# Attention weights of two score blocks added into one square ahead of the transpose and taken apart by a mask behind it

## The chip, the cores and the metric

The kernel runs on one core of a Trainium2 chip. The core has a matrix engine (TensorE, PE), which reads its stationary operand with separate weight loads (PEld), a vector engine (VectorE, DVE), an activation engine (ScalarE, ACT), a general engine (GpSimd, POOL), and a sync engine (SyncE, SP) whose queue issues most of the transfers. Each engine works through its own instructions in order and waits for the others at semaphores. The metric is the time of one execution on the device in microseconds (us).

## The reference, cut to what matters

The program is one layer of a hybrid decoder, for a prompt of 512 tokens and 8 samples of 4 tokens, all in f32. One large input projection feeds two branches, an mLSTM and a sliding-window attention; both are gated, projected, added, projected again and normalised. The change touches only the attention of the prompt: 32 query heads of 64 in 4 key groups, a window of 128 tokens, blocks of 128 queries. A query block sees its own key block and the one ahead of it.

```python
def _swa_prompt(q, k, v, slopes, sinks):
    ...
    kk = jnp.concatenate([jnp.pad(kb, pad)[:, :-1], kb], axis=2)
    vv = jnp.concatenate([jnp.pad(vb, pad)[:, :-1], vb], axis=2)
    qi = jnp.arange(WINDOW)[:, None]
    kj = jnp.arange(2 * WINDOW)[None, :]
    dist = qi + WINDOW - kj
    valid = (dist >= 0) & (dist < WINDOW) & ((blk > 0) | (kj >= WINDOW))
    out = _sink_attend(qb, kk, vv, dist, valid, slopes, sinks)
```

`_sink_attend` takes the scaled scores less slope x distance, a softmax over them and one sink logit, and multiplies by the values. From `dist`: query i sees key j of the block ahead only for j > i, and key j of its own block only for j <= i. So of the 256 weights of a query in two blocks, each column j holds one that can differ from zero: in the block ahead if j > i, in the own block if j <= i.

## The kernel before, in words

All large products are made in f32 precision from two halves: a value is split into a rounded high part (cast by ACT, L200 or L243) and the remainder (subtracted by DVE, L201 or L244), and three products hi x hi, hi x lo, lo x hi are summed (L664, L666).

The input projection runs in `paired`: two column tiles of 128 are computed together by seven half products (`half_product`, steps n = 0 to 6), each 24 matmuls of 128 x 272 columns. The loop prepares weights up to three steps ahead (`prepare`: a sum of weight tiles by DVE at L644, or by an accumulating transfer that POOL issues at L642, then the split at L200 and L201 into buffers of two), gathers finished banks (`gather`, L674 to L693, one of them on POOL at L683), and then calls `tick()`, which resumes every side task once. Side tasks are generators: each piece of work up to the next `yield` is written down behind one half product, and `tick` orders the PE instructions of a side task behind the last matmul of that half product. The Tile framework lays the instructions of each engine into one order with a planner that simulates times; preparations and gathers have a higher priority (`AHEAD`), side tasks the plain one.

The attention of the prompt is such a side task (`attentions`, `attention`). It handles two heads (a = 0, 1) at a time, 16 times; one such turn k takes the queries of one pair of projected tiles (`end_qz`) and is spread over the steps of the next two pairs, 14 steps:

- scores (L772, PE) for four query blocks: `s_` is 128 queries x 4 blocks x 256, columns 0 to 127 for the key block ahead, 128 to 255 for the own one; block 0 has only the own one. DVE adds slope x distance (`nb`, scaled by ACT at L762) and finds the minimum (L774);
- exponentials with row sums (L783, ACT), the sink's (L784), the reciprocal (L785, L786, DVE), and the scaling by it (L789, ACT);
- seven transposes a head (L800, PE) of 128 x 128 blocks, in two PSUM tiles of four and three, and their split into `ph` and `pl` (L243, ACT; L244, DVE);
- the product with the values (L810, PE): four pairs of matmuls, whose columns are the own block b and, for b below 3, the block ahead of query block b + 1, so `p_[:, 2b:2b+2]`;
- the sum of its two halves (L813, ACT; L814, DVE) into `hT`, and, after both heads, the product with the gate `sz` (L816, POOL) and the store. `sz` has one buffer and is written for the next turn at L840.

The yields of a turn: one behind each head's scores, one empty, one behind each head's exponentials and scaling, one empty, then for each head transposes, yield, yield, value product, and a last yield ahead of L816.

Of the kernel before, what the change touches and what calls it, by code (L numbers as in the profile page):

```python
# [16 lines left out]
F32R = mybir.dt.float32r  # L17
AF = mybir.ActivationFunctionType
ALU = mybir.AluOpType
# [23 lines left out]
C_ID, C_TRI, C_M8, C_SM, C_SEL, C_M2, C_DIST, C_SB, C_Q, C_N = 0, 128, 256, 264, 296, 328, 330, 586, 718, 846  # L43
# [25 lines left out]
def build(tc, nc, i, o, dbg=None):  # L69
    es = ExitStack()  # L70
    with es:
        _build(tc, nc, i, o, es)


def _build(tc, nc, i, o, es):
# [3 lines left out]
    def pool(stack, name, bufs, space=None, side=None):  # L79
        kw = {"space": space} if space is not None else {}  # L80
        if space is None:
            kw["side"] = side or "right"
            kw["reuse_waits"] = "tile"
        return stack.enter_context(tc.tile_pool(name=name, bufs=bufs, **kw))

    y_p, y_s, C_p, n_p, m_p, kb_p, vb_p, C_s, n_s, m_s, kb_s, vb_s = o
    V, A, G, PE = nc.vector, nc.scalar, nc.gpsimd, nc.tensor
# [13 lines left out]
    def nm(s):  # L101
        count[0] += 1
        return f"{s}_{count[0]}"

    def sm():
        return psB.tile([128, 512], F32, tag="sm", name=nm("sm"))
# [4 lines left out]
    def r32(ap):  # L111
        return ap.bitcast(F32)
# [4 lines left out]
    def blk(ap, n=4):  # L117
        return ap.rearrange("p (b x) -> p b x", b=n)
# [23 lines left out]
    cc = cst.tile([128, C_DIST], F32, name="cc")  # L142
# [3 lines left out]
    ident = cc[:, C_ID:C_ID + 128]  # L146
# [95 lines left out]
    def hilo(src, hi, lo, eng=None):  # L242
        A.copy(hi, src)  # L243
        (eng or V).tensor_tensor(out=lo, in0=src, in1=r32(hi), op=ALU.subtract)  # L244
# [54 lines left out]
    for c0, n in ((0, 256), (256, 256), (512, 512), (1024, 512), (1536, 512)):  # L299
        if c0 < 1536:  # L300
            t_ = xr.tile([128, 4, n], F32, tag=f"x{n}", name=nm("xr"))[:]
        else:
            t_ = act2.tile([128, 8, HT], F32, tag="act", name=nm("xr"))[:].rearrange("p a b -> p (a b)")
            t_ = blk(t_[:, 0:4 * n])
# [10 lines left out]
    for g in range(8):  # L315
        for q in range(2):
            k = g * 2 + q
            pt = sm()
# [408 lines left out]
    bp = {}  # L727

    def open_attention():
        for name, bufs in (("b1", 1), ("bs", 2), ("bt", 1), ("bq", 2), ("bm", 2)):  # L730
            bp[name] = pool(esB, name, bufs)

    def btile(p, shape, tag, dt=F32):
        return bp[p].tile(shape, dt, tag=tag, name=nm(tag))

    def scores_tile():
        return btile("bs", [128, 4, 256], "s")
# [16 lines left out]
    def attention(k, qs, sz, kv):  # L754


        k1, k2, VA = kv
        hT = btile("b1", [128, SEQ], "hT")
        st = []
        for a in range(2):  # L760
            nb = btile("b1", [128, 256], f"nb{a}")
            A.activation(nb[:], state["ca"][:, 0:256], AF.Copy, scale=SLOPES[2 * k + a])  # L762
            s_ = scores_tile()
            mx, mn, sums = (btile("bm", [128, 4], t_) for t_ in ("mx", "mn", "sums"))
            h = slice(2 * k + a, 2 * k + a + 1)
            for j in range(4):
                if j % 2 == 0:
                    pp = sm()
                w0 = 128 if j == 0 else 0
                c0, k0 = (j % 2) * 256, max(j - 1, 0) * 128  # L770
                for n, kx in enumerate((k1, k2)):
                    PE.matmul(pp[:, c0 + w0:c0 + 256], qs[a][:, j * 128:j * 128 + 128], kx[:, k0:k0 + 256 - w0],  # L772
                              start=(n == 0), stop=(n == 1))
                V.tensor_tensor_reduce(s_[:, j, w0:256], pp[:, c0 + w0:c0 + 256], nb[:, w0:256], 1.0, nsinkb[:, h],  # L774
                                       ALU.add, ALU.min, accum_out=mn[:, j:j + 1])
            st.append((s_, mx, mn, sums, h))
            yield
        yield
        for a in range(2):
            s_, mx, mn, sums, h = st[a]  # L780
            for j in range(4):
                sj = s_[:, j, 128 if j == 0 else 0:256]
                A.activation(sj, sj, AF.Exp, bias=mn[:, j:j + 1], scale=-1.0, accum_out=sums[:, j:j + 1])  # L783
            A.activation(mx[:], mn[:], AF.Exp, bias=sinkb[:, h])  # L784
            V.tensor_tensor(out=sums[:], in0=sums[:], in1=mx[:], op=ALU.add)  # L785
            V.reciprocal(sums[:], sums[:])  # L786
            for j in range(4):
                sj = s_[:, j, 128 if j == 0 else 0:256]
                A.activation(sj, sj, AF.Copy, scale=sums[:, j:j + 1])  # L789
            yield  # L790
        yield
        for a in range(2):
            s_ = st[a][0]

            ph, pl = (btile("bt", [128, 7, 128], t_, F32R) for t_ in ("ph", "pl"))
            for m0_, m1_ in ((0, 4), (4, 7)):
                pt = sm()
                for m in range(m0_, m1_):
                    b, own = m // 2, m % 2 == 0
                    PE.transpose(pt[:, (m - m0_) * 128:(m - m0_) * 128 + 128],  # L800
                                 s_[:, b, 128:256] if own else s_[:, b + 1, 0:128], ident)
                n = m1_ - m0_
                hilo(blk(pt[:, 0:n * 128], n), ph[:, m0_:m1_], pl[:, m0_:m1_])
            yield
            yield
            po = sm()
            for b in range(4):
                n = 256 if b < 3 else 128
                for m, p_ in enumerate((ph, pl)):
                    PE.matmul(po[:, b * 128:b * 128 + n], VA[:, b], p_[:, 2 * b:2 * b + n // 128],  # L810
                              start=(b == 0 and m == 0), stop=(b == 3 and m == 1), skip_group_check=True)
            rows_ = slice(a * 64, a * 64 + 64)
            A.copy(hT[rows_], po[64:128])  # L813
            V.tensor_tensor(out=hT[rows_], in0=po[0:64], in1=hT[rows_], op=ALU.add)  # L814
        yield
        G.tensor_tensor(out=hT[:], in0=sz[:, 0:SEQ], in1=hT[:], op=ALU.mult)  # L816
        nc.sync.dma_start(d_bra[k][:, 0:SEQ], hT[:])

# [36 lines left out]
    def attentions():  # L855
# [10 lines left out]
        with tc.issue_after(state["load"].ins):  # L866
            nc.sync.dma_start(state["ca"][:], i["consts"][:, C_DIST:C_DIST + 388])
        open_attention()
        state["open"] = True
        spawn(old_rows())  # L870
        for k in range(16):
            if k % 4 == 0:
                kv = kv_head(k // 4)
            while k not in waiting:
                yield
            yield
            yield
            yield from attention(k, *waiting.pop(k), kv)
            state["done"] = k + 1
# [487 lines left out]
    ph = wA1.tile([128, 1280], F32R, name="ph")  # L1367
    pl = wA1.tile([128, 1280], F32R, name="pl")
# [526 lines left out]
```

## Time and profile before

| What | us |
|---|---|
| median of 3 runs | 2493.77 |
| lowest and highest | 2491.63, 2494.89 |
| the profiled execution | 2497.55 |
| its span, first to last instruction | 2495.7 |
| PE busy | 2453.8 |
| DVE busy | 1817.8 |
| ACT busy | 1244.1 |
| POOL busy | 373.1 |

The profile is of one execution. The busy time of an engine is the time in which at least one of its instructions runs; matmuls overlap, so the mean duration of one is longer than the spacing from one to the next. In a row of groups stand the line, engine and operation, output and inputs, the shapes and the number of instructions, then the merged busy time in us and the mean duration in ns, and the idle time of the engine just ahead of them with what ended it. In a row in order of time stand the start, the duration in us (from the first start to the last end, if several are merged, xN), and in brackets an idle time ahead of it.

### The profile page before, as it was taken

The page shows a single profiled execution, that of the slowest core. Times are in us where ns is not written, and L with a number is a line of the kernel's source. Part 1 is how long each engine was busy: PE and PEld are TensorE (multiplying, and loading weights), DVE is VectorE, ACT ScalarE, POOL GpSimd, SP SyncE. Part 2 cuts the span into 40 slices and gives each one's busy share as a digit, 9 for nine tenths or more (in the row PEclk, how much of TensorE's full clock was granted, in tenths as well). Part 3 has the DMA queues.
Part 4 walks back from the last instruction along what each step waited for, and adds up shares of the span by engine and source line. Part 5 has one row for each costly group of instructions (what it writes and reads, how often), then busy time and mean ns, then how long its engine had stood idle before and what let it go on. Part 6 is the DMA issues. An engine that isn't in the chain of part 4 may idle for free. (4 is left out here: it accounts for less than half of the span.)

```text
span 2495.7 us, 48772 instructions
## 1 busy us (share of the span) xinstructions
PE 2453.8 (98%) x19542; PEld 2394.0 (96%) x19542; DVE 1817.8 (73%) x2785; ACT 1244.1 (50%) x2033; POOL 373.1 (15%) x376
## 2 busy tenths in 40 slices
PE   8999999999999999999999999999999999999997
PEld 8999999999999999989999999999999999999997
DVE  7867677677677677777878788878855654666667
ACT  6457677667667665433433444444633333334431
POOL 2111121121111111121021121210000000110111
PEclk9999999999999999999999999999999999999999
DMA  6677666656666655468678677677755546788776
GB/s 166 154 185 187 150 151 159 158 144 163 153 152 156 151 128 151 106 204 243 205 216 243 167 232 240 188 225 226 251 171 172 189 149 205 198 229 258 213 220 190
DMA packets 557172, 464.71 MB, mean 186 GB/s; under 512 B 45328, under 2 KB 454080, under 8 KB 556688
## 3 DMA queue, kind: packets, MB, share of 16 engines
q1 hardware_dynamic: 540048, 402.07, 54.4%
q0 software_dynamic: 15696, 57.15, 11.8%
q8 instruction: 154, 2.52, 0.4%
q10 hardware_dynamic: 1200, 2.36, 0.3%
q14 instruction: 74, 0.61, 0.1%
HBM read 319.06 MB, written 96.31 MB: 166 GB/s over the span
## 5 line engine op out<-in xcount | busy, mean ns | idle before, releaser
L200 ACT CAST wh<-raw 128x1024 fp32r<-128x1024 f32 x632 | 661.9, 1048 | 814.6 <-PE bank L664 663.8
L201 DVE TENSOR_TENSOR wl<-raw,wh 128x1024 fp32r<-128x1024 f32 x632 | 778.9, 1234 | 222.7 <-ACT wh L200 203.4
L664 PE MATMUL bank<-xk,wh 128*128 128x272 f32 x2336 | 325.0, 290 | 0.9 <-DVE ev L689 0.9
L644 DVE TENSOR_TENSOR raw<-raw,raw 128x1024 f32<-128x1024 f32 x238 | 304.5, 1280 | 17.3 <-DMA raw<-in_w_in 8.2
L664 PEld LDWEIGHTS bank<-xk,wh 128*128 128x128 f32 x2336 | 304.3, 189 | 4.2 <-issue 2.6
L683 POOL TENSOR_TENSOR ev<-p,ev 128x272 f32<-128x272 f32 x82 | 124.8, 1522 | 674.1 <-ACT ev L682 613.7
L666 PE MATMUL bank<-xk,wl 128*128 128x272 f32 x1168 | 172.4, 288 | 0.8 <-DVE wl L201 0.8
L664 PE MATMUL bank<-s1h,wh 128*128 128x272 f32 x656 | 169.1, 291 | 0.2 <-ACT wh L200 0.2
L664 PE MATMUL bank<-n3h,wh 128*128 128x272 f32 x656 | 169.1, 289 | 0.0
L664 PE MATMUL bank<-n2h,wh 128*128 128x272 f32 x656 | 168.2, 289 | 0.6 <-ACT wh L200 0.6
L664 PE MATMUL bank<-s4h,wh 128*128 128x272 f32 x656 | 168.3, 290 | 0.1
L664 PE MATMUL bank<-n3l,wh 128*128 128x272 f32 x656 | 167.9, 287 | 0.0
L664 PE MATMUL bank<-n2l,wh 128*128 128x272 f32 x656 | 167.5, 287 | 0.0
L664 PE MATMUL bank<-s1l,wh 128*128 128x272 f32 x656 | 167.2, 287 | 0.0
L664 PE MATMUL bank<-s4l,wh 128*128 128x272 f32 x656 | 167.0, 287 | 0.0
L666 PEld LDWEIGHTS bank<-xk,wl 128*128 128x128 f32 x1168 | 156.6, 188 | 1.1 <-DVE wl L201 1.0
L664 PE MATMUL bank<-a11h,wh 128*128 128x272 f32 x584 | 150.8, 290 | 2.6 <-ACT wh L200 2.5
L209 PE MATMUL bank<-bh,wl 128*128 128x272 f32 x704 | 148.5, 291 | 4.7 <-DVE wl L201 4.7
L664 PE MATMUL bank<-a11l,wh 128*128 128x272 f32 x584 | 149.6, 289 | 0.0
L209 PE MATMUL bank<-bh,wh 128*128 128x272 f32 x704 | 148.8, 290 | 0.0
L209 PE MATMUL bank<-bl,wh 128*128 128x272 f32 x704 | 148.6, 290 | 0.0
L664 PEld LDWEIGHTS bank<-n3h,wh 128*128 128x128 f32 x656 | 123.3, 188 | 1.9 <-issue 1.4
(488 smaller groups left out, 5515.4 us busy)
## 6 DMA issues: line engine op xcount, KB each, us to landing
raw<-in_w_in SPq DMA_DIRECT2D x296, 512.0 KB
raw<-raw POOLq DMA_DIRECT2D x90, 512.0 KB, 5.0
C<-in_state_mlstm_C SPq DMA_DIRECT2D x32, 1024.0 KB
out<-C SPq DMA_DIRECT2D x64, 512.0 KB
raw<-in_w_proj_a SPq DMA_DIRECT2D x32, 512.0 KB
raw<-in_w_proj_m SPq DMA_DIRECT2D x32, 512.0 KB
raw<-in_w_out SPq DMA_DIRECT2D x32, 512.0 KB
d_v<-ev SPq DMA_DIRECT2D x16, 272.0 KB
```

Of the source, the lines that this page charges most:

```text
L200: A.copy(wh[:, k:k + n], raw[:, k:k + n])
L201: V.tensor_tensor(out=wl[:, k:k + n], in0=raw[:, k:k + n], in1=r32(wh[:, k:k + n]), op=ALU.subtract)
L209: PE.matmul(ps[f][:, :w], a[:, kk], b(k, c, w), start=(k == 0 and n == 0), stop=(k == 15 and n == 2))
L644: V.tensor_tensor(out=w[out][:], in0=w[a][:], in1=w[b][:], op=ALU.add)
L664: PE.matmul(ps, wh[:, k], x(p, k), start=(first and k == 0 and p == 0), stop=False, skip_group_check=True)
L666: state["end"] = PE.matmul(ps, wl[:, k], x(0, k), start=False, stop=(k == 7), skip_group_check=True)
L683: G.tensor_tensor(out=c22, in0=p1, in1=c11, op=ALU.subtract)
```

## The change

Ahead of the scaling, POOL adds the weights of the key block ahead to those of the own block, for query blocks 1 to 3: one square of 128 x 128 a query block. Only that square is scaled, and only four transposes a head are made, into one PSUM tile. Behind them, ACT writes the rounded copy `fh` and DVE the remainder `fl` over the free halves of `s_`. A tile of ones and zeros (`upper`, one exponential of the triangle constant when the pools are opened) takes them apart: the product with it is the own block's part (f x 1 or f x 0), and the difference of the square and that product is the part of the block ahead. POOL does this for `fh`, DVE for `fl`, into tiles `P`, of which there are three buffers for the four of a turn. The tiles go to the same value products as before. The copies of the distances for the two heads (`nb`) now share one buffer. The transposes of both heads now stand in two steps that follow each other, and each head's value product one step later than before; the last yield ahead of the gate's product is gone.

```diff
-        for name, bufs in (("b1", 1), ("bs", 2), ("bt", 1), ("bq", 2), ("bm", 2)):
+        for name, bufs in (("b1", 1), ("bs", 2), ("bt", 3), ("bq", 2), ("bm", 2)):
             bp[name] = pool(esB, name, bufs)
+        upper = bp["upper"] = btile("b1", [128, 128], "upper")
+        A.activation(upper[:], cc[:, C_TRI:C_TRI + 128], AF.Exp)
...
-            nb = btile("b1", [128, 256], f"nb{a}")
+            nb = btile("b1", [128, 256], "nb")
...
+            G.tensor_tensor(out=s_[:, 1:4, 128:256], in0=s_[:, 1:4, 0:128], in1=s_[:, 1:4, 128:256], op=ALU.add)
             A.activation(mx[:], mn[:], AF.Exp, bias=sinkb[:, h])
             V.tensor_tensor(out=sums[:], in0=sums[:], in1=mx[:], op=ALU.add)
             V.reciprocal(sums[:], sums[:])
             for j in range(4):
-                sj = s_[:, j, 128 if j == 0 else 0:256]
+                sj = s_[:, j, 128:256]
                 A.activation(sj, sj, AF.Copy, scale=sums[:, j:j + 1])
             yield
         yield
+        ps_ = []
         for a in range(2):
             s_ = st[a][0]
-
-            ph, pl = (btile("bt", [128, 7, 128], t_, F32R) for t_ in ("ph", "pl"))
-            for m0_, m1_ in ((0, 4), (4, 7)):
-                pt = sm()
-                for m in range(m0_, m1_):
-                    b, own = m // 2, m % 2 == 0
-                    PE.transpose(pt[:, (m - m0_) * 128:(m - m0_) * 128 + 128],
-                                 s_[:, b, 128:256] if own else s_[:, b + 1, 0:128], ident)
-                n = m1_ - m0_
-                hilo(blk(pt[:, 0:n * 128], n), ph[:, m0_:m1_], pl[:, m0_:m1_])
-            yield
+            pt = sm()
+            for b in range(4):
+                PE.transpose(pt[:, b * 128:b * 128 + 128], s_[:, b, 128:256], ident)
+            fh, fl = s_[:, :, 0:128], s_[:, :, 128:256]
+            A.copy(fh.bitcast(F32R), blk(pt[:]))
+            V.tensor_tensor(out=fl.bitcast(F32R), in0=blk(pt[:]), in1=fh, op=ALU.subtract)
+
+            up = bp["upper"][:].unsqueeze(1).to_broadcast([128, 4, 128])
+            both = []
+            for e, f in ((G, fh), (V, fl)):
+                p_ = btile("bt", [128, 7, 128], "P", F32R)
+                e.tensor_tensor(out=p_[:, 0:7:2], in0=f, in1=up, op=ALU.mult)
+                e.tensor_tensor(out=p_[:, 1:7:2], in0=f[:, 1:4], in1=r32(p_[:, 2:7:2]), op=ALU.subtract)
+                both.append(p_)
+            ps_.append(both)
+            yield
+        for a in range(2):
             yield
             po = sm()
             for b in range(4):
                 n = 256 if b < 3 else 128
-                for m, p_ in enumerate((ph, pl)):
+                for m, p_ in enumerate(ps_[a]):
                     PE.matmul(po[:, b * 128:b * 128 + n], VA[:, b], p_[:, 2 * b:2 * b + n // 128],
                               start=(b == 0 and m == 0), stop=(b == 3 and m == 1), skip_group_check=True)
             rows_ = slice(a * 64, a * 64 + 64)
             A.copy(hT[rows_], po[64:128])
             V.tensor_tensor(out=hT[rows_], in0=po[0:64], in1=hT[rows_], op=ALU.add)
-        yield
+            if a == 0:
+                yield
         G.tensor_tensor(out=hT[:], in0=sz[:, 0:SEQ], in1=hT[:], op=ALU.mult)
```

## The prediction

> **What bounds the kernel now.** I read the first two parts of the page, then the busy time of each engine over the stretch in which the attention runs, then the waits of that stretch, then single instructions in order of time.
>
> ```profile
> span 2495.7 us, 48772 instructions
> ...
> PE 2453.8 (98%) x19542; PEld 2394.0 (96%) x19542; DVE 1817.8 (73%) x2785; ACT 1244.1 (50%) x2033; POOL 373.1 (15%) x376
> ...
> PEclk9999999999999999999999999999999999999999
> ```
>
> TensorE (PE) is busy 98% of the span at full granted clock. The changed code runs only from about 186 to 930 us, so that stretch decides. The columns of the next row are the stretch, its length, and the busy time and number of instructions of PE, its weight loads, DVE, ACT and POOL.
>
> ```profile
> core 0: us, PE busy (x) PEld busy (x) DVE busy (x) ACT busy (x) POOL busy (x), PEclk, DMA share, GB/s
> 186.00:930.00 744.00, 744.00 (x6003) 744.00 (x6003) 541.18 (x867) 512.44 (x942) 134.95 (x107) 1.00 0.64 155
> ```
>
> PE has no gap at all: 6003 matmuls in 744.00 us, one every 0.124 us. So a step of 24 matmuls (one half product) takes 0.124 x 24 = 2.98 us. DVE stands idle for 744 - 541 = 203 us, ACT for 232 us, POOL for 609 us. The waits of the same stretch have no row in which PE waits; the others wait, mostly for PE:
>
> ```profile
> POOL hT L816 <- issue: 154.9, 15, 11.2
> POOL raw L642 <- DVE sums L785: 142.8, 13, 11.3
> ACT wh L200 <- PE bank L664: 140.8, 107, 2.0
> DVE wl L201 <- ACT wh L200: 70.1, 55, 1.6
> ...
> ACT sz L840 <- POOL hT L816: 4.9, 6, 0.8
> ```
>
> The largest real wait is ACT's: the cast of the next weights (L200) waits for PE to free the buffer. The work around PE runs ahead of it and is throttled by it. Here, then, an instruction taken from PE shortens the kernel by the time until the next matmul can start, and work added elsewhere is free until it uses up the lead.
>
> **The change part by part.**
>
> *Transposes.* Three of seven go in each of 32 heads: 96 of 224. Their price must be the spacing on PE, not the duration, since matmuls overlap.
>
> ```profile
> 198.68 0.93 PE L800 MATMUL sm<-cc,s 128*128 128x128 f32 x7
> ...
> 245.06 1.16 PE L666 MATMUL bank<-a11h,wl 128*128 128x272 f32 x8
> 246.06 0.92 PE L800 MATMUL sm<-cc,s 128*128 128x128 f32 x7
> 246.75 0.37 PE L664 MATMUL bank<-s1h,wh 128*128 128x272 f32 x1
> 246.96 0.29 PE L664 MATMUL bank<-s1l,wh 128*128 128x272 f32 x1
> ```
>
> The first row is the batch of one query block earlier. Seven transposes begin at 246.06 and the next matmul at 246.75: 0.69 / 7 = 0.099 us each. The longer first gap of the matmuls behind (0.21 instead of 0.125 us) is paid once per batch, and the number of batches stays 32. Three fewer: 0.30 us a head, 32 x 0.30 = 9.5 us. The grouped row bounds it from above:
>
> ```profile
> L800 PE MATMUL sm<-cc,s 128*128 128x128 f32 x224 | 30.0, 274 | 0.0
> L800 PEld LDWEIGHTS sm<-cc,s 128*128 128x128 f32 x224 | 24.8, 140 | 0.0
> ```
>
> The merged busy time of the group is 30.0 us, with the tail of each batch in it: 30.0 / 224 x 96 = 12.9 us. Nearest is the spacing, and I take 9.5 us.
>
> The Trainium skill (TensorE: Matmul & The Clock Gate, Part 4: PE-mode transpose) gives about 275 ns for one transpose in a kernel's context, and the 274 ns mean here agrees; by that figure the 96 would be worth an estimated 26 us. Behind other matmuls the spacing in the rows is 99 ns, and the sum goes by that.
>
> *Copy and subtract behind the transposes.* ACT's casts and DVE's subtractions were two of each a head, 512 and 384 wide; now one of each, 512 wide. The scaling of the weights becomes 128 wide in all four blocks. Then the two masked halves: a product of 512 and a difference of 384, for the high part on POOL and for the low part on DVE.
>
> ```profile
> L789 ACT ACTIVATE s<-s,sums 128x256 f32<-128x256 f32 x96 | 41.4, 494 | 0.0
> ...
> L244 DVE TENSOR_TENSOR pl<-sm,ph 128x512 fp32r<-128x512 f32 x32 | 22.0, 688 | 0.0
> ...
> L243 ACT CAST ph<-sm 128x512 fp32r<-128x512 f32 x32 | 18.8, 587 | 1.0
> ...
> L244 DVE TENSOR_TENSOR pl<-sm,ph 128x384 fp32r<-128x384 f32 x32 | 17.5, 548 | 0.0
> L243 ACT CAST ph<-sm 128x384 fp32r<-128x384 f32 x32 | 15.6, 487 | 0.0
> ...
> L789 ACT ACTIVATE s<-s,sums 128x128 f32<-128x128 f32 x32 | 12.7, 396 | 3.7 <-DVE sums L786 3.7
> ...
> L244 DVE TENSOR_TENSOR t<-t,t x16: 682/687/694, 1803.7 to 1996.3; 128x512 fp32r<-128x512 f32 x16
> ```
>
> ACT loses 0.487 (the second cast) + 3 x (0.494 - 0.396) = 0.78 us a head, 25 us in all. DVE loses 0.548 and gains a product of 512 out of SBUF (0.687, the last row) and a difference of 384 (0.548, the same width out of PSUM): +0.69 us a head, 22 us in all, against 203 us idle. Cost on PE's path: nothing, covered by those idle shares; without the cover DVE's 22 us would be paid.
>
> *POOL.* Three operations a head: the sum of the two score blocks (384), the product (512), the difference (384). Bounds from rows of POOL with little or no company, and one in company:
>
> ```profile
> 14.92 1.34 POOL L346 TENSOR_TENSOR r<-n2r,r 128x544 f32<-128x544 f32 x1 [13.56 <-ACT r L328]
> ...
> 117.24 0.78 POOL L683 TENSOR_TENSOR ev<-p,ev 128x272 f32<-128x272 f32 x1 [7.82 <-ACT ev L682]
> ...
> 215.82 2.31 POOL L816 TENSOR_TENSOR hT<-sz,hT 128x512 f32<-128x512 f32 x1 [10.43 <-DVE hT L814]
> ```
>
> 272 wide takes 0.78, 544 wide 1.34 us: 2.06 ns an element and 0.22 us fixed, so 384 costs 1.01 and 512 costs 1.27 us, 3.3 us a head and 105 us in all. The row of 512 took 2.31 us, by which the three would cost 2.31 x (1280 / 512) = 5.8 us a head, 185 us in all. Both fit into 609 idle us; I take 3.3 to 5.8. The 2.31 us has a reason that DVE shows at the same time:
>
> ```profile
> 215.76 1.23 DVE L644 TENSOR_TENSOR raw<-raw,raw 128x1024 f32<-128x1024 f32 x1
> 217.31 0.44 DVE L691 SCALAR_TENSOR_TENSOR ev<-bank,ev 128x272 f32<-128x272 f32 x1 [0.32 <-PE bank L666]
> 217.67 1.55 DVE L201 TENSOR_TENSOR wl<-raw,wh 128x1024 fp32r<-128x1024 f32 x1
> ```
>
> The DVE addition with two SBUF inputs (215.76 to 216.99) delays POOL, which ends at 218.13, 1.14 us behind it. In turn the DVE subtraction of 217.67, also with two SBUF inputs, lasts 1.55 us where the usual is 1.22: 0.33 us of waiting for POOL. The DVE operation of 217.31, with one input in PSUM, shows none. So POOL's new work costs DVE between 0 and 3.3 us a head; from the row, some 0.33 us per POOL operation, 1.0 us a head, 32 us in all. With the 22 us that makes 54 of 203 idle us: hidden.
>
> *How much lead is there?* The tightest spot that I found is ahead of the transposes:
>
> ```profile
> 243.74 1.03 ACT L200 CAST wh<-raw 128x1024 fp32r<-128x1024 f32 x1
> ...
> 245.32 1.05 ACT L200 CAST wh<-raw 128x1024 fp32r<-128x1024 f32 x1
> ...
> 244.80 1.22 DVE L201 TENSOR_TENSOR wl<-raw,wh 128x1024 fp32r<-128x1024 f32 x1 [1.11 <-ACT wh L200]
> ```
>
> ACT writes the weights for the step after the transposes at 243.74 to 244.78, and PE wants them at 246.75: 2.0 us of lead. DVE's low part is done at 246.03 and wanted 16 matmuls later, at 246.75 + 16 x 0.125 = 248.75: 2.7 us. ACT is the fuller one here:
>
> ```profile
> 226.13:236.00 9.87, 9.87 (x82) 9.87 (x81) 7.27 (x22) 8.34 (x23) 2.64 (x2) 1.00 0.46 101
> 236.00:246.05 10.05, 10.05 (x82) 10.05 (x81) 7.40 (x10) 10.02 (x19) 0.86 (x1) 1.00 0.87 230
> ```
>
> The fourth busy time of a row is ACT's: 8.34 of 9.87 us, then 10.02 of 10.05 us. Its scaling (L789) will now wait for POOL's sum behind the exponentials, 1.0 to 2.3 us later than today at worst; against it stand the 1.5 us idle before, the shorter scaling, and the 2.0 us of lead. I take nothing; without cover it is up to 2.3 us a head.
>
> *Order and buffers.* The number of steps of an attention stays eleven, so no query pair waits longer for its turn. The second head's transposes move one step earlier, to one step behind the first's; head 0's value products move one step later, and so do head 1's:
>
> ```profile
> 213.17 0.28 PE L810 MATMUL sm<-ph,VA 128*128 128x256 f32 x1
> ```
>
> They start at 213.17 now and would at about 216.2 less the saving. So POOL's final product (L816) starts at about 218.8 instead of 215.82, and behind it the next gate (L840, one buffer), which waits 4.9 us in 6 places already, could hold ACT up to 3 us more, 16 times; the cast of weights queued behind it has about the lead above. POOL's accumulating transfers (L642) can fall behind one head's product and difference, 2.3 us:
>
> ```profile
> 204.54 0.86 POOL L642 DMA_DIRECT2D raw<-raw  x1
> ...
> 212.36 1.05 ACT L200 CAST wh<-raw 128x1024 fp32r<-128x1024 f32 x1 [1.55 <-PE bank L664]
> ...
> raw<-raw POOLq DMA_DIRECT2D x90, 512.0 KB, 5.0
> ```
>
> The one issued at 204.54 lands some 5.0 us after it was issued, by 210.4, and ACT casts these data at 212.36: 2.0 us of lead and ACT's own lead behind it. I take nothing for the gate and the transfers. No other transfer changes: the output of a head pair on SP's queue leaves 3 us later and is read only after the stage.
>
> The fourth of the P tiles has three buffers to live in: DVE's last product and difference of a pair wait for the value products of head 0 to end, and the next split (L201) may be queued behind them. Bounds: 0 if DVE's order puts them behind that moment, 2.98 us (one step) if ahead of it. They then have two steps before head 1 needs them, 6 us for 1.2 us of work. I take 0. With one buffer for the scaled distances, ACT's copy for head 1 waits for head 0's last score, and head 1's first score for the copy: up to one cast of ACT ahead of it (1.05 us) a pair. Both lie some ten steps ahead of the transposes that need them; I take 0. The triangle's exponential is a single instruction outside the loop; I leave it at 0.
>
> **Sum.** 2497.55 us is the time of the profiled execution (span 2495.7 and 1.9 us around it). Minus 9.5 gives 2488.0. The median of the runs is 3.8 us below the profiled one, so the forecast for it is 2493.77 - 9.5 = 2484.3, say 2484: faster by 0.4%. What remains behind 930 us is as PE-bound (98%), so the gain is carried to the end.
>
> **The rivals.**
>
> *POOL holds DVE (slower).* Place: the two or three steps around the transposes, where POOL's product and difference fall among DVE's splits. If 0.33 us of waiting for each of three POOL operations a head came through to PE, that is 1.0 us a head, 32 us - 9.5 = 22 us slower, 2516 us. It decides from 0.30 us a head reaching PE. For it: the 1.55 us row, and the DVE work added at the same place. Against: 2.7 us of lead and 203 us of idle DVE. The Trainium skill (SBUF — State Buffer, SBUF: two separate sides) states an exclusive lock between the two, held for the whole instruction; the rows agree.
>
> *A wait replaces the gain (same).* ACT's scaling waits for POOL's sum, or its gate for POOL's final product, in about one head of three by 1 us more than the lead: 32 / 3 x 1 = 10.7 us, and the time stays at 2494 to 2496. For it: ACT at 10.02 of 10.05 us. Against: it has less work than before.
>
> *Full price of a transpose (faster).* If each gave back its 274 ns, 96 x 0.274 = 26 us, 2467. Against it: the spacing above.
>
> **How the numbers follow.** The forecast has 0.64, POOL holding DVE 0.19, the wait that cancels 0.13, the full price 0.04. Differences below 0.2% (5 us) can't be told from none here. Faster is 0.64 + 0.04 = 0.68, same 0.13, slower 0.19. The likeliest one's own range is 2481 (12.9 us gained) to 2489 (half of it lost); both signs hold a good share, so the range runs to 2504, which is the cancelling wait and the lower half of the slower rival, and starts at 2480: the full price and the upper half of the slower rival stay out, 0.14 together.
>
> **What would show it.** Right: 128 transposes at L800's successor with the same 0.1 us spacing, PE still without waits in the stretch, the period between two query blocks (47.38 us now, from the batches of transposes at 198.68 and 246.06) shorter by 0.6 us, POOL busier by 105 to 185 us, ACT less busy by 25, DVE more by 22 to 54. Wrong: rows in which PE waits for L200 or L201 in the stretch, splits of 1.5 us and more in number, ACT's scaling waiting for POOL, or value products that wait for the P tiles.

## The result, and the profile after

| | median us | runs |
|---|---|---|
| before | 2491.86 (2488.45 to 2496.28) | 14 |
| changed | 2484.39 (2480.24 to 2490.88) | 14 |

The ratio is 0.9972, with a 95% interval of 0.9965 to 0.9979: 7.0 us faster, between 5.2 and 8.7; the medians differ by 7.5 us. The forecast was 2484 and 9.5 us.

The first lines of the page of the changed kernel:

```profile
span 2478.7 us, 48809 instructions
...
PE 2441.8 (99%) x19446; PEld 2382.2 (96%) x19446; DVE 1892.3 (76%) x2817; ACT 1219.5 (49%) x2002; POOL 508.3 (21%) x472
...
PEclk9999999999999999999999999999999999999998
```

The profiled execution took 2480.46 us, 17 us less than the one of before. That is more than the medians differ by, and most of the surplus is scatter, as will be seen. PE stays busy in every slice, now 99%; DVE rose from 73% to 76%, POOL from 15% to 21%, ACT fell from 50% to 49%.

The busy times in a stretch that lies inside the attention in both, 186 to 900 us (stretch, length, then PE, its weight loads, DVE, ACT and POOL with their numbers of instructions); first before:

```profile
186.00:900.00 714.00, 714.00 (x5761) 714.00 (x5761) 517.12 (x838) 495.93 (x915) 131.19 (x105) 1.00 0.64 156
```

then changed:

```profile
186.00:900.00 714.00, 714.00 (x5748) 714.00 (x5747) 595.72 (x879) 478.83 (x897) 258.44 (x197) 1.00 0.66 158
```

PE has no gap in either. DVE gained 79 us, POOL 127 us, ACT lost 17 us. The waits of the changed kernel in the attention (waiting engine and line, releaser, us in all, times, longest) have again no row of PE:

```profile
ACT wh L200 <- PE bank L664: 151.9, 107, 2.0
...
DVE wl L201 <- ACT wh L200: 40.1, 39, 1.5
...
ACT wh L200 <- DMA raw<-raw: 13.2, 6, 3.2
ACT s L792 <- DVE sums L789: 12.2, 16, 0.8
ACT sz L851 <- POOL hT L827: 7.4, 7, 1.9
```

ACT still waits for PE above all, so the lead is there. The scaling (L792) waits 12.2 us in 16 places, the gate (L851) 7.4 us, and the casts wait 13.2 us in 6 places for POOL's accumulating transfers, which the list of before has no row for. Not in the rows above: ACT's copy of the distances into the one `nb` waits 19.3 us in 15 places for head 0's last score, and DVE 7.3 us behind it. Nothing of all this reaches PE.

A batch of transposes on PE, in order of time:

```profile
196.17 1.16 PE L666 MATMUL bank<-a11h,wl 128*128 128x272 f32 x8
197.17 0.60 PE L800 MATMUL sm<-cc,s 128*128 128x128 f32 x4
197.52 0.37 PE L664 MATMUL bank<-s1h,wh 128*128 128x272 f32 x1
197.73 0.29 PE L664 MATMUL bank<-s1l,wh 128*128 128x272 f32 x1
```

Four transposes begin at 197.17, the next matmul at 197.52: 0.35 us where seven took 0.69. So the three that went are worth 0.34 us a head, 0.113 us each, and not three times the batch's mean of 0.099.

The next turn's batch of the first head:

```profile
243.88 0.60 PE L800 MATMUL sm<-cc,s 128*128 128x128 f32 x4
```

From 197.17 to 243.88 it is 46.71 us, where before took 47.38 (198.68 to 246.06, the rows of the prediction, which calls it the period between two query blocks; it is one turn of two heads). In the mean of the first 14 turns it is 46.72 against 47.36, so the change gains 0.64 us a turn, 10.2 us in 16 turns. The prediction named 0.6 us as a sign of being right.

For the time of the whole attention I use one instruction that both kernels have once in every pair of column tiles: ACT's gather of the first bank (L674). It occurs 82 times; numbers 6 and 36, counted from 0, lie near the first and the last batch of transposes. In the profile before:

```profile
198.89 0.39 ACT L674 ACTIVATE p<-bank 128x272 f32<-128x272 f32 x1
...
910.18 0.40 ACT L674 ACTIVATE p<-bank 128x272 f32<-128x272 f32 x1
```

and changed:

```profile
197.79 0.39 ACT L674 ACTIVATE p<-bank 128x272 f32<-128x272 f32 x1
...
898.23 0.40 ACT L674 ACTIVATE p<-bank 128x272 f32<-128x272 f32 x1
```

From 6 to 36 it is 910.18 - 198.89 = 711.29 us before and 898.23 - 197.79 = 700.44 us changed: 10.85 us less. The sum said 9.5. Not all of it is gain: in the new order, seven matmuls of the main loop come behind gather 36 instead of ahead of it. The next two rows count the matmuls into a bank (PE's x) in the stretch behind, from gather 36 to gather 40, before and changed:

```profile
910.18:1008.69 98.51, 86.28 (x667) 84.13 (x668) 6.98 (x16) 4.72 (x13) 1.00 0.48 130
...
898.23:999.17 100.94, 87.56 (x674) 85.09 (x675) 6.98 (x16) 4.77 (x12) 1.00 0.47 129
```

At 0.125 us each they are 0.9 us, by which 6 to 36 looks shorter and 36 to 40 longer. The turn above is free of this.

The added work cost DVE more than I had set. The groups of the changed kernel that show it:

```profile
L201 DVE TENSOR_TENSOR wl<-raw,wh 128x1024 fp32r<-128x1024 f32 x222 | 286.3, 1289 | 41.0 <-ACT wh L200 40.1
...
L809 POOL TENSOR_TENSOR P<-s,upper 128x512 fp32r<-128x512 f32 x32 | 59.8, 1869 | 88.3 <-ACT s L802 88.3
...
L810 POOL TENSOR_TENSOR P<-s,P 128x384 fp32r<-128x384 f32 x32 | 45.9, 1433 | 1.3
...
L786 POOL TENSOR_TENSOR s<-s 128x384 f32<-128x384 f32 x31 | 35.1, 1131 | 125.1 <-issue 64.3 <-ACT s L785 60.9
...
L788 DVE TENSOR_TENSOR sums<-sums,mx 128x4 f32<-128x4 f32 x31 | 29.3, 944 | 0.0
L810 DVE TENSOR_TENSOR P<-s,P 128x384 fp32r<-128x384 f32 x32 | 28.7, 897 | 0.5
...
L809 DVE TENSOR_TENSOR P<-s,upper 128x512 fp32r<-128x512 f32 x32 | 28.0, 876 | 0.6
```

and the two of before to compare with:

```profile
L201 DVE TENSOR_TENSOR wl<-raw,wh 128x1024 fp32r<-128x1024 f32 x220 | 272.2, 1237 | 70.6 <-ACT wh L200 70.1
...
L785 DVE TENSOR_TENSOR sums<-sums,mx 128x4 f32<-128x4 f32 x32 | 5.0, 155 | 0.0
```

The sum of four columns (L785, now L788) went from 155 to 944 ns, though it works on four elements a row as before. In order of time, POOL's sums and DVE's:

```profile
230.90 1.01 POOL L786 TENSOR_TENSOR s<-s 128x384 f32<-128x384 f32 x1 [3.64 <-ACT s L785]
236.34 1.23 POOL L786 TENSOR_TENSOR s<-s 128x384 f32<-128x384 f32 x1 [4.43 <-issue]
...
231.03 0.90 DVE L788 TENSOR_TENSOR sums<-sums,mx 128x4 f32<-128x4 f32 x1
...
236.62 0.97 DVE L788 TENSOR_TENSOR sums<-sums,mx 128x4 f32<-128x4 f32 x1
```

POOL's sums run from 230.90 to 231.91 and from 236.34 to 237.57; the tiny sums, which have both inputs in SBUF, end at 231.93 and 237.59, that is, when POOL ends. It is the waiting that the 1.55 us row of before showed, now 31 times in place of a 0.155 us instruction: 25 us. Two of the experiments below confirm it: with the masking on DVE and the sum left on POOL the row stays long (first row, all_dve), with the sum on DVE too it is back at 155 ns (second row, no_pool).

```profile
L788 DVE TENSOR_TENSOR sums<-sums,mx 128x4 f32<-128x4 f32 x31 | 29.9, 965 | 0.0
...
L788 DVE TENSOR_TENSOR sums<-sums,mx 128x4 f32<-128x4 f32 x32 | 5.0, 155 | 0.0
```

The splits (L201) take 0.052 us more on average, 11.5 us in 222.

### The profile page after: what moved, and what is told of

Read it like the earlier page. It is cut to its first block, busy times and chain, and to the rows that moved or that the text cites. A ratio compares the mean times of both kernels' runs of the same rounds, so it can differ in the third digit from the quotient of the medians.

```text
span 2478.7 us, 48809 instructions
## 1 busy us (share of the span) xinstructions
PE 2441.8 (99%) x19446; PEld 2382.2 (96%) x19446; DVE 1892.3 (76%) x2817; ACT 1219.5 (49%) x2002; POOL 508.3 (21%) x472
## 4 chain that ended last, share of the span: by engine, by line
PE 85%; DMA 5%; issue 5%; DVE 4%; ACT 1%; SPq 0%; POOL 0%; DVEq 0%; POOLq 0%; ACTq 0%
PE bank L664 45%; PE bank L666 22%; PE bank L209 6%; PE sm L1410 2%; PE sm L1442 1%; PE bank L1222 1%; PE sm L774 1%; PE sm L1455 1%; PE sm L820 1%; DMA tx<-d_y 1%; DVE wl L201 1%; DMA ty<-d_y 1%; PE sm L1772 1%; DMA raw<-in_w_in 1%; PE sm L1227 1%
## 5 line engine op out<-in xcount | busy, mean ns | idle before, releaser
L201 DVE TENSOR_TENSOR wl<-raw,wh 128x1024 fp32r<-128x1024 f32 x632 | 791.3, 1253 | 191.6 <-ACT wh L200 166.8
L644 DVE TENSOR_TENSOR raw<-raw,raw 128x1024 f32<-128x1024 f32 x238 | 303.0, 1274 | 10.9 <-DMA raw<-in_w_in 5.1
L683 POOL TENSOR_TENSOR ev<-p,ev 128x272 f32<-128x272 f32 x82 | 119.2, 1454 | 467.6 <-ACT ev L682 422.2
L642 POOL DMA_DIRECT2D raw<-raw x90 | 78.5, 872 | 290.3 <-DVE ev L691 172.3
```

Source lines behind the costliest of these rows:

```text
L201: V.tensor_tensor(out=wl[:, k:k + n], in0=raw[:, k:k + n], in1=r32(wh[:, k:k + n]), op=ALU.subtract)
L642: G.dma_start(out=w[out][:], in_=w[b][:], accum_op=ALU.add)
L644: V.tensor_tensor(out=w[out][:], in0=w[a][:], in1=w[b][:], op=ALU.add)
L683: G.tensor_tensor(out=c22, in0=p1, in1=c11, op=ALU.subtract)
```

## The experiments

All were timed in five rounds (the repeat of before in three) against the kernel before on the same chip.

| Kernel | median us | before | ratio and interval |
|---|---|---|---|
| t_only | 2484.08 | 2493.58 | 0.9962 (0.9949 to 0.9976) |
| plus3 | 2496.46 | 2493.58 | 1.0015 (1.0003 to 1.0026) |
| all_dve | 2483.28 | 2493.58 | 0.9958 (0.9942 to 0.9973) |
| pool_twice | 2500.57 | 2493.58 | 1.0028 (1.0016 to 1.0040) |
| after_again | 2486.15 | 2492.97 | 0.9971 (0.9960 to 0.9981) |
| no_pool | 2485.73 | 2492.97 | 0.9973 (0.9964 to 0.9983) |
| all_dve_again | 2483.71 | 2492.97 | 0.9964 (0.9952 to 0.9977) |
| before_again | 2491.92 | 2492.97 | 0.9996 (0.9986 to 1.0005) |
| early_values | 2483.72 | 2494.48 | 0.9959 (0.9945 to 0.9972) |
| early_values_dve | 2484.23 | 2494.48 | 0.9955 (0.9942 to 0.9969) |
| after_third | 2485.59 | 2494.49 | 0.9958 (0.9944 to 0.9973) |
| early_values_again | 2484.33 | 2494.49 | 0.9961 (0.9947 to 0.9976) |

Each run has a profile, and the starts of the gather L674 cut them into the same stretches of work. The lengths in us, each the difference of two such starts; the column 6 to 44 is the whole from the first transposes to well behind the attention:

| Profile | 6 to 36 | 36 to 40 | 6 to 44 | 44 to 72 | 72 to 81 |
|---|---|---|---|---|---|
| before | 711.29 | 98.51 | 915.15 | 652.91 | 638.89 |
| before_again | 711.29 | 99.32 | 914.90 | 652.75 | 632.42 |
| changed | 700.44 | 100.94 | 905.99 | 651.75 | 633.65 |
| after_again | 700.44 | 101.69 | 906.87 | 652.34 | 633.47 |
| after_third | 700.44 | 101.44 | 908.09 | 652.50 | 632.99 |
| t_only | 701.07 | 98.24 | 905.35 | 652.34 | 634.21 |
| plus3 | 710.06 | 103.11 | 917.22 | 651.55 | 637.38 |
| all_dve | 700.45 | 101.02 | 905.03 | 651.85 | 632.76 |
| all_dve_again | 700.45 | 101.10 | 904.77 | 652.45 | 637.01 |
| no_pool | 701.71 | 101.35 | 907.87 | 651.57 | 635.64 |
| pool_twice | 714.77 | 102.81 | 921.02 | 653.44 | 633.95 |
| early_values | 701.14 | 98.98 | 904.53 | 651.48 | 633.82 |
| early_values_again | 701.15 | 98.88 | 905.37 | 652.20 | 634.99 |
| early_values_dve | 701.04 | 98.48 | 904.12 | 652.65 | 635.38 |

The attention itself repeats to 0.01 us from profile to profile of one kernel. The long stretch from 72 to 81, plain products that the change doesn't touch, scatters by 6 us: 638.89 and 632.42 for the same program. The new order of steps (all kernels here but before, before_again and t_only) has the seven matmuls, 0.9 us, in the column 36 to 40 instead of 6 to 36. So the texts below also give the turn: the mean of the first 14 times from one batch of the first head's transposes to the next.

**The transposes alone (t_only).** The kernel before, with four transposes of a head in place of seven and the rest as it was; the last three blocks of the weights are copies of others.

```diff
-            for m0_, m1_ in ((0, 4), (4, 7)):
-                pt = sm()
-                for m in range(m0_, m1_):
-                    b, own = m // 2, m % 2 == 0
-                    PE.transpose(...)
+            pt = sm()
+            for m in range(4):
+                b, own = m // 2, m % 2 == 0
+                PE.transpose(...)
+            for m0_, m1_ in ((0, 4), (4, 7)):
                 n = m1_ - m0_
                 hilo(blk(pt[:, 0:n * 128], n), ph[:, m0_:m1_], pl[:, m0_:m1_])
```

> The kernel before with three of the seven transposes of a head left out and nothing else changed: one PSUM tile of four transposes, whose columns are used a second time for the last three blocks of the weights, so three blocks of each head are copies of others and the attention is not the reference's. Same casts, same subtractions, same places of the steps. Theory (PE is the only bound in the attention, a transpose costs its spacing of 0.10 to 0.11 us, everything else of the change is hidden): 9.5 to 11 us below before, no wait of PE in the stretch, the turn of the attention at about 46.7 us instead of 47.4. Rival (a transpose costs more of its 274 ns, and the rest of the change gives a part of it back): 14 us or more below before.

The median fell by 9.5 us, and 6 to 36 by 711.29 - 701.07 = 10.2 us. In that stretch lie 30 of the 32 batches, 210 transposes before and 120 in t_only, so it is 0.114 us for each of 90, and 10.9 us for all 96. The turn says the same: 46.68 us against 47.36, 0.68 us for six. 6 to 44 fell by 9.7 us. No wait of PE in the stretch. The theory's size; the full duration of a transpose is out.

**All but the transposes (plus3).** The changed kernel with the three transposes put back into a tile that nothing reads.

```diff
                 PE.transpose(pt[:, b * 128:b * 128 + 128], s_[:, b, 128:256], ident)
+            pt2 = sm()
+            for b in range(1, 4):
+                PE.transpose(pt2[:, b * 128:b * 128 + 128], s_[:, b, 128:256], ident)
```

> The changed kernel with three more transposes a head, into a second PSUM tile that nothing reads: PE has its old number of 224 transposes, all else is the change. Theory: within 2 us of before, since what POOL, DVE and ACT do is hidden, and the turn of the attention is 47.4 us again. Rival (the work on POOL and DVE or the new order costs PE some of its gain): 3 us or more above before.

The median is 2.9 us above before, by the ratio between 0.7 and 6.5 us: between the theory's 2 and the rival's 3, so the time doesn't tell them apart. The profile tells where: the turn is 47.37 us against 47.36, so the rest of the change costs PE nothing inside the attention (6 to 36, 710.06 against 711.29 us, is shorter mostly by the seven matmuls). Behind it 36 to 40 takes 103.11 against 98.51 and 99.32 us, 2.9 to 3.7 us more when the 0.9 us are taken off. The rival was right that there is a cost, and its place is not where I had looked.

**No masking on POOL (all_dve, all_dve_again).**

```diff
-            for e, f in ((G, fh), (V, fl)):
+            for e, f in ((V, fh), (V, fl)):
```

> The changed kernel with the masked product and the difference of the high part on DVE too; only the sum ahead of the scaling stays on POOL. POOL loses about 106 us of busy time, DVE gains 32 x (0.68 + 0.54) = 39 us of its own and loses waits. Theory (lead covers both ways): within 2 us of the changed kernel. Rival (POOL and DVE holding each other costs PE): 3 us or more faster than the changed kernel. If DVE becomes the bound instead, PE waits for L201 and it is slower by more than 3 us.

> The changed kernel with the high part's product and difference on DVE, once more on the same chip as the changed kernel and the one with nothing on POOL. Theory: within 2 us of the changed kernel. Rival: 3 us or more faster than it, as the two medians of different chips suggest (10.3 us below before against 7.5).

Inside the attention it is 700.45 in both, 0.01 us from the changed kernel: POOL and DVE holding each other costs PE nothing. The medians, 10.3 and 9.3 us below before, are 2 to 3 us better than the changed kernel's (7.5 on another chip, 6.8 on the same one), and their intervals overlap with its; 6 to 44 differs by 1 to 3 us, all of it behind gather 40 (from 40 to 44, 103.56 and 103.22 us against 104.61, 104.74 and 106.21), where the masking no longer runs and the rows show a granted clock of 0.98 against 0.97; as far as gather 40 it is 801.5 us against 801.4 to 802.1. Whether it is faster stays open, and the profiles show no gain in the attention. DVE's groups and busy time:

```profile
L809 DVE TENSOR_TENSOR P<-s,upper 128x512 fp32r<-128x512 f32 x64 | 42.3, 682 | 0.0
...
L810 DVE TENSOR_TENSOR P<-s,P 128x384 fp32r<-128x384 f32 x64 | 37.9, 613 | 0.0
```

```profile
186.00:900.00 714.00, 714.00 (x5748) 714.00 (x5747) 605.54 (x939) 479.74 (x897) 159.56 (x136) 1.00 0.66 158
```

Twice as many products and differences, each at 682 and 613 ns instead of 876 and 897: DVE's busy time rises by 605.5 - 595.7 = 10 us for 39 us of moved work, mostly since these and the splits (1257 instead of 1289 ns) no longer meet POOL's masking.

**Nothing on POOL (no_pool).** As all_dve, and the sum of the two blocks on DVE too.

```diff
-            G.tensor_tensor(out=s_[:, 1:4, 128:256], ...
+            V.tensor_tensor(out=s_[:, 1:4, 128:256], ...
```

> The changed kernel with all three of its POOL operations on DVE (sum, product and difference of the high part). DVE gets 32 x (0.55 + 0.68 + 0.54) = 57 us and loses its waits for POOL, among them those of the 4-wide sum at L788 (0.94 us each now, 0.155 before: 25 us). Theory: PE is still the bound, within 2 us of the changed kernel. Rival (waiting between POOL and DVE, or ACT behind POOL's sum, still costs PE): 3 us or more faster than the changed kernel. If DVE is too full: PE waits for L201 and it is slower by 3 us or more.

2485.73 beside 2486.15 of the changed kernel on the same chip: no difference. Inside the attention it is 701.71 us, 1.3 more than the changed kernel, 0.9 of it in a single turn (47.63 us). So neither ACT's scaling behind POOL's sum nor the long L788 costs anything at the end that the times can show.

**POOL's masking twice (pool_twice).**

```diff
-                e.tensor_tensor(out=p_[:, 0:7:2], in0=f, in1=up, op=ALU.mult)
-                e.tensor_tensor(out=p_[:, 1:7:2], in0=f[:, 1:4], in1=r32(p_[:, 2:7:2]), op=ALU.subtract)
+                for _ in range(2 if e is G else 1):
+                    e.tensor_tensor(out=p_[:, 0:7:2], in0=f, in1=up, op=ALU.mult)
+                    e.tensor_tensor(out=p_[:, 1:7:2], in0=f[:, 1:4], in1=r32(p_[:, 2:7:2]), op=ALU.subtract)
```

> The changed kernel with POOL's masked product and difference done twice over, the same values written again: POOL gets 32 more products (1.87 us each) and differences (1.43 us each), about 105 us. Theory: still hidden, less than 3 us above the changed kernel, no row of PE waiting for L200 or L201 in the stretch. Rival (POOL is near the point where it decides): PE waits in the stretch, for the P tiles or for weights, and 10 us or more above the changed kernel, up to 105.

7.0 us above before, 14 to 16 us above the changed kernel's distance from it. PE's waits in the attention, where no other kernel here has more than one of 0.2 us:

```profile
PE bank L664 <- DVE ev L689: 6.7, 11, 1.4
PE bank L666 <- DVE wl L201: 2.4, 2, 1.5
```

From 6 to 36 it takes 914.43 - 199.66 = 714.77 us by the same gathers, 14.3 more than the changed kernel; PE is busy for 705.0 us of it, so 9.8 us are idle time and the rest has no row. The theory fell at twice the work: PE waits for DVE, for a bank that a gather (L689) should have emptied and for the low parts of weights. Two things hold DVE back there. Its splits take longer (1289 ns in the changed kernel), and it now waits for the value products to free one of the three P buffers, a wait that the changed kernel doesn't have:

```profile
L201 DVE TENSOR_TENSOR wl<-raw,wh 128x1024 fp32r<-128x1024 f32 x217 | 313.6, 1447 | 26.4 <-ACT wh L200 24.9
...
DVE P L810 <- PE sm L821: 14.5, 14, 1.3
```

So PE can be made to wait for DVE, and the point where it starts lies between one and two times the masking that the change gave POOL. How much of it is POOL holding DVE, the slower rival's mechanism, and how much the missing fourth P buffer, this run does not separate.

**The changed kernel and the kernel before once more (after_again, before_again).**

> The changed kernel as it is, once more, beside the kernel before on the same chip. In the first profile the attention gained 10.3 to 10.9 us while the medians differ by 7.5. Theory (the gain of the attention reaches the end, and the difference is the scatter of the runs): 8 to 11 us below before. Rival (2 to 4 us are given back behind the attention every time): 5 to 7.5 us below before, and the pairs right behind the attention start later against before than the last ones in it.

> The kernel before, for a second profile. Theory: its turn of the attention is 47.4 us as in the first profile, and its stretch behind the attention, 1586 us in the first profile from the last batch of transposes to the end, differs from that by several us, since the program is the same and its runs scatter by 8 us. Rival: that stretch agrees within 2 us, and what the changed kernel's profile gained there is the change's.

6.8 us below before: the rival's range. 6 to 36 is 700.44 again, and 36 to 40 is 101.69 us against 99.32. Before's second profile has the same 711.29 us in the attention, and the stretch from 72 to 81 is 6.5 us shorter than in its first, as before_again's theory said. A part of that has a row; the waits of PE from 1765 to 2170 us, in the first profile of before:

```profile
PE bank L209 <- DVE wl L201: 4.7, 2, 4.0
```

and in the second:

```profile
PE bank L209 <- DVE wl L201: 0.7, 1, 0.7
```

One wait of 4.0 us for a split came and went with the program unchanged. The other 2.5 us stand in the column of the granted clock. In the first profile, right behind that wait, it is half for 6.8 us:

```profile
2150.30:2157.10 6.80, 5.03 (x22) 5.03 (x23) 5.42 (x8) 1.37 (x2) 0.94 (x1) 0.50 0.81 164
```

From 72 to 81 PE is busy for 634.13 us in the first profile and for 631.59 us in the second, with the same number of matmuls: 2.5 us, half of the 5.03 us of this row. The second profile shows 1.00 there. Hence the 17 us between the first two profiles: 1.1 ahead of gather 6, 10.85 from 6 to 36, 2.4 given back from 36 to 40, 5.2 from 72 to 81, and smaller pieces.

**The value products a step earlier (early_values, early_values_again, early_values_dve).** What costs 2 us behind the attention? Of the edits, the transposes alone don't bring it (t_only: 98.24 us from 36 to 40), and all kernels with the new order of steps have it (100.9 to 103.1). So the old steps of the value products were put back into the changed kernel:

```diff
             ps_.append(both)
             yield
         for a in range(2):
-            yield
             po = sm()
...
+            yield
             if a == 0:
                 yield
         G.tensor_tensor(out=hT[:], in0=sz[:, 0:SEQ], in1=hT[:], op=ALU.mult)
```

> The changed kernel with the value products back at the steps of the kernel before: head 0's two steps behind its transposes, head 1's two steps later, and a step between these and POOL's final product. In two profiles of the changed kernel, from the last gather of the attention to four pairs behind it took 100.9 and 101.7 us, against 98.5 and 99.3 us before. Theory (the last output of the attention comes a step later, so the work behind it, which waits for its memory, starts late): 98 to 99.5 us there, and 1 to 3 us faster than the changed kernel, as long as PE doesn't wait for the P tiles. Rival (the loss comes from elsewhere, or is scatter): 101 us or more there, and no faster than the changed kernel.

> The same with the high part's product and difference on DVE: both heads' P tiles now come from one engine, within two steps. Theory: as fast as the one with POOL, or up to 2 us faster, 10 to 12 us below before. Rival (DVE can't write four P tiles in time for the earlier value products): PE waits for them at the value products, about 1 us a pair, and it is 10 us or more slower than the other.

36 to 40 is 98.98 us, and 98.48 with the masking on DVE: the loss is gone. Both kernels have the same number of matmuls there as the changed kernel, so the seven that moved play no part. PE waits nowhere in the attention, so the P tiles are there in time a step earlier, too, even all from DVE. SP's queue behind the last store of the attention, in after_again:

```profile
923.34 0.34 SPq L828 DMA_DIRECT2D d_bra<-hT  x1
924.43 0.37 SPq L635 DMA_DIRECT2D raw<-in_w_in  x1
924.89 0.53 SPq L908 DMA_DIRECT2D gas<-d_bra  x1
925.47 2.80 SPq L909 DMA_DIRECT2D kas<-d_ka  x1
...
934.33 0.60 SPq L918 DMA_DIRECT2D kb<-in_state_attn_k  x1
```

and in early_values:

```profile
919.11 0.34 SPq L828 DMA_DIRECT2D d_bra<-hT  x1
919.54 0.39 SPq L908 DMA_DIRECT2D gas<-d_bra  x1
919.98 1.43 SPq L909 DMA_DIRECT2D kas<-d_ka  x1
...
927.30 0.60 SPq L918 DMA_DIRECT2D kb<-in_state_attn_k  x1
```

Gather 36 is at 900.64 in the one and at 900.45 in the other, so, counted from there, the last store (L828) comes 4.0 us earlier with the early value products, and the keys of the samples (kb) are asked for 6.8 us earlier: in after_again a load of weights (L635) stands between the store and the loads, and the issue of kas takes 2.80 instead of 1.43 us. From 36 to 40, PE is busy for 99.53 of 101.69 us in after_again and for 98.83 of 98.98 us in early_values. So 2.0 of the 2.7 us between the two are idle time of PE; for the other 0.7 us I have no row. Its waits in after_again:

```profile
PE bank L664 <- DVE ev L685: 0.8, 1, 0.8
PE sm L935 <- DMA kb<-in_state_attn_k: 0.8, 1, 0.8
PE sm L952 <- ACT kT L937: 0.3, 1, 0.3
PE sm L935 <- DVE E L955: 0.3, 1, 0.3
```

The wait for kb, 0.8 to 1.2 us, is in all eight profiles of kernels with the late value products, masking on either engine, and in none of the others. So the order of steps is shown to be the cause of the loss; that it acts through the late store and the loads behind it is shown for the wait for kb, and for the rest only likely.

The last pair put both on one chip:

> The changed kernel as it is, a third time, beside the one with the earlier value products on the same chip. Theory: from the last gather of the attention to four pairs behind it 101 to 102 us again, 6 to 8.5 us below before. Rival (that loss is scatter): 98 to 100 us there.

> The changed kernel with the value products one step earlier, once more on the same chip as the changed kernel. Theory: 98 to 99.5 us in the same place, and 1 to 4 us faster than the changed kernel, 8.5 to 11 us below before. Rival: no faster than the changed kernel within 1 us.

36 to 40: 101.44 and 98.88 us, as expected. The medians are 8.9 us below before, where 6 to 8.5 was expected for the changed kernel, and 10.2 us. They differ by 1.3 us, less than the scatter; as far as gather 44 the profiles show early_values ahead (6 to 44: 904.53 and 905.37 against 905.99, 906.87 and 908.09); whether that reaches the end is not settled by the times. Against before its medians are 10.8 and 10.2 us lower.

## Why the prediction was right

*What bounds.* PE was the bound and stayed it. No row of PE waiting in the attention, before or after.

*Transposes.* The spacing, not the duration, was the price: 0.114 us each by t_only, 10.9 us, where I had 0.099 and 9.5. The term was 1.4 us too small because a batch's mean was used for its last three; the upper bound of 12.9 held. The changed kernel's turn gained 0.64 us, not t_only's 0.68, so 10.2 us; for the 0.04 us a turn between them I have no row. The rival of the full duration (26 us) is out by t_only.

*Copy, subtract, POOL.* All hidden, by plus3 (a turn of 47.37 against 47.36 us), all_dve and no_pool. ACT lost 17 us in the stretch of equal length and 24.6 us over the whole span, where 25 was said. POOL's 127 us (135 over the span) lie in the 105 to 185. DVE's 22 to 54 us were 79 (75 over the span): the term for DVE waiting for POOL, 32 us, was too small, above all since the four-column sum L788 was not in it (25 us). The cover was 203 us, so it changed nothing.

*POOL holds DVE.* It is real, by L788 in no_pool, and it didn't decide. At twice the masking PE waits for DVE, in part perhaps for want of a P buffer. The Trainium skill (SBUF — State Buffer, SBUF: two separate sides) says that the one that starts first keeps the shared port for its whole instruction and the other stops; L788 ends with POOL's sum to 0.02 us, which agrees.

*A wait replaces the gain.* Not in its place: ACT's scaling waits 12.2 us, the gate 7.4 us, the casts 13.2 us for transfers (the 2.0 us of lead that I gave them were used up, and a cast waited up to 3.2 us more), and PE none.

*Order and buffers.* Here a step failed. I said of the later output only that it is "read only after the stage" and took nothing. The attention of the samples loads behind that last store, and the three profiles of the changed kernel take 2.0 to 2.8 us more from 36 to 40 than the two of early_values, which has the same number of matmuls there. So from 6 to 44 the change gains 7 to 9 us, not 10, which is what the medians show (7.5, 6.8 and 8.9). That the forecast of 2484 met the median of 2484.39 is luck: the gain was put 2.0 us too high, and the median of before on which it stood was 1.9 us higher than that of the 14 runs. Within the gain, too, two errors go against each other, a transpose priced too low and this cost set to zero.

The one `nb` makes ACT wait, as the prediction said it could (19.3 us in 15 places, 1.3 us at most), and neither it nor the fourth P tile makes PE wait. Whether four buffers and two copies would help is untried.

## What to carry to other kernels

Where the matrix engine has no gap, price a removed instruction by the spacing of its neighbours, and for the last of a batch by the difference of two batches, not by a batch's mean. Work moved to other engines was free here while they ran ahead; doubling a part of it in an experiment showed how near the limit is. And when a step moves, follow its last output past the end of its own stage: here value products one step later, with a store that nobody in the stage reads, cost 2 us behind it. When a trace is cut at an instruction, count the work between the cuts: seven matmuls that changed sides looked like 0.9 us of gain on one side and of loss on the other.

## What was unexpected

A DVE addition of four elements a row went from 0.155 to 0.944 us because POOL had begun a sum in SBUF just ahead of it: it ended when POOL did, and was short again where POOL had no sum. And the static order of a kernel reproduces a stretch of 700 us to 0.01 us in three profiles, while a stretch with one late split and a few microseconds at half the granted clock differs by 6 us between two executions of the same program.
